# Moving one load and one store of a rotary kernel from SyncE's queue to GpSimd's

## The chip, the cores and the metric

One core of one Trainium2 chip. The metric is device time in microseconds (us) of one execution; executions of one kernel mostly agree within about 0.3%. "Faster" or "slower" means by more than 2%.

A word on names. Tile 0 to 3 are the four quarters of x, 8.39 MB each. "Load 1" brings tile 1 into on-chip memory, "store 1" takes it back. A "row" is what one partition contributes to one transfer: 64 KB for a whole tile, 32 KB for half a tile. Each of the 16 DMA engines carries 8 of the 128 rows of every transfer. A "hole" is time in which the DMA engines have nothing to move. A "packet record" is the trace's entry for one piece that a DMA engine moved: its queue, start, duration and size. "The software queue" is GpSimd's, "the hardware queue" is SyncE's.

## The reference

```python
def reference(x, cos, sin):          # x (16, 512, 16, 64), cos and sin (512, 32), float32
    x1, x2 = x[..., :32], x[..., 32:]
    cos = cos[None, :, None, :]; sin = sin[None, :, None, :]
    first  = x1[..., :16] * cos[..., :16] - x1[..., 16:] * sin[..., :16]
    second = x1[..., :16] * sin[..., :16] + x1[..., 16:] * cos[..., :16]
    return np.concatenate([first, second, x2], axis=-1)
```

x2, half of the data, only passes through: 33.55 MB in, 33.55 MB out, and little arithmetic.

## The kernel before

A ring of three slots of 64 KB per partition holds the tiles; tile 3 reuses the slot of tile 0, so load 3 must wait until store 0 has landed. VectorE rotates each tile in place, in two halves of K/2 = 8 positions. All x transfers are issued by SyncE, in one queue.

```python
    NS = 3; KC = K // 2; KL = 14
    ring = const_pool.tile([P, NS, K, H, D], fp32)

    def load(t, lo=0, hi=K):
        return nc.sync.dma_start(out=rows(t, lo, hi), in_=xf[t, :, lo * R : hi * R])
    def store(t, lo=0, hi=K):
        return nc.sync.dma_start(out=of[t, :, lo * R : hi * R], in_=rows(t, lo, hi))

    nc.gpsimd.dma_start(out=spread[:, 0, 0], in_=cosf)
    nc.gpsimd.dma_start(out=spread[:, 0, 1], in_=sinf)
    load(0)
    load(1)
    load(2, 0, KC)
    # ... VectorE spreads cos and sin over the partitions ...
    def rotate(t, lo, hi):
        # ... views x1, c, s, b_t ...
        nc.vector.tensor_mul(out=b_t, in0=x1, in1=s)
        nc.vector.tensor_mul(out=x1, in0=x1, in1=c)
        nc.vector.tensor_sub(...)
        nc.vector.tensor_add(...)
    def turn(t):
        rotate(t, 0, KC)
        rotate(t, KC, K)
        return store(t)

    turn(0)
    load(2, KC, K)
    near = load(3, 0, KL)
    load(3, KL, K)
    tc.add_manual_dep(turn(1).ins, near.ins.name, ...)   # store 1 waits for load 3
    turn(2)
    turn(3)
```

## Time and profile before

| | before |
|---|---|
| median of all its runs | 161.5 to 161.7 us |
| span in the trace | 160.33 us |
| DMA packets, share of 16 engines' span | 97.8% |
| VectorE busy | 70% |
| VectorE's last instruction ends | 130.58 us |
| last store lands | 159.29 us |

The prediction below shows the lines that carry this. Two more, from the waits and the DMA issues of the kernel before. In the first the columns are who waited, for whom, us in total, times, longest; in the second the transfer, the number of issues and the median us from issue to landing (KB each stands only where a transfer is not a whole tile):

```profile
DVE b_t L96 <- DMA ring<-in_x_dram: 1.9, 1, 1.9
```
```profile
out_dram<-ring SPq DMA_DIRECT2D x4, 25.6
```

VectorE waits for x once, for load 0, and never again: every later tile is there early. A store takes 25.6 us to land where its bytes alone need 19.5, since others stand before it in the queue.

### The profile page before, as it was taken

The page shows a single profiled execution, that of the slowest core. Times are in us where ns is not written, and L with a number is a line of the kernel's source. Part 1 is how long each engine was busy: PE and PEld are TensorE (multiplying, and loading weights), DVE is VectorE, ACT ScalarE, POOL GpSimd, SP SyncE. Part 2 cuts the span into 40 slices and gives each one's busy share as a digit, 9 for nine tenths or more (in the row PEclk, how much of TensorE's full clock was granted, in tenths as well). Part 3 has the DMA queues.
Part 4 walks back from the last instruction along what each step waited for, and adds up shares of the span by engine and source line. Part 5 has one row for each costly group of instructions (what it writes and reads, how often), then busy time and mean ns, then how long its engine had stood idle before and what let it go on. Part 6 is the DMA issues. An engine that isn't in the chain of part 4 may idle for free.

```text
span 160.3 us, 113 instructions
## 1 busy us (share of the span) xinstructions
DVE 112.4 (70%) x43; POOL 1.4 (1%) x6
## 2 busy tenths in 40 slices
DVE  1000959999999999999999999999999950000000
POOL 3000000000000000000000000000000000000000
DMA  7969969699699996999999995996996996996990
GB/s 262 540 262 540 491 294 523 278 507 491 294 392 441 474 523 262 523 392 392 499 482 458 458 444 253 546 523 262 523 523 262 523 507 278 523 507 278 523 507 16
DMA packets 1504, 67.24 MB, mean 419 GB/s; under 512 B 192, under 2 KB 192, under 8 KB 224
## 3 DMA queue, kind: packets, MB, share of 16 engines
q1 hardware_dynamic: 1440, 67.11, 97.6%
q0 software_dynamic: 64, 0.13, 0.2%
HBM read 33.69 MB, written 33.55 MB: 419 GB/s over the span
## 4 chain that ended last, share of the span: by engine, by line
DVE 59%; DMA 14%; issue 7%; DVEq 1%
DVE b_t L96 22%; DVE ring L97 22%; DMA ring<-in_x_dram 14%; DVE ring L101 10%; DVE ring L98 4%; DVEq L148 1%; DVEq L96 0%
## 5 line engine op out<-in xcount | busy, mean ns | idle before, releaser
L96 DVE TENSOR_TENSOR b_t<-ring,table 128x4096 f32<-128x4096 f32 x8 | 35.5, 4432 | 2.1 <-DMA ring<-in_x_dram 1.9
L97 DVE TENSOR_TENSOR ring<-ring,table 128x4096 f32<-128x4096 f32 x8 | 35.4, 4424 | 0.3
L98 DVE TENSOR_TENSOR ring<-ring,b_t 128x2048 f32<-128x2048 f32 x8 | 18.3, 2287 | 0.3
L101 DVE TENSOR_TENSOR ring<-ring,b_t 128x2048 f32<-128x2048 f32 x8 | 18.2, 2280 | 0.0
L73 DVE LOAD_MASK_SELECT spun<-stage x1 | 0.0, 14 | 14.4 <-DMA stage<-in_sin_dram 14.4
L83 DVE COPY table<-packed 32x1024 f32<-32x1024 f32 x4 | 2.7, 684 | 0.1
L80 DVE COPY packed<-spun 32x512 f32<-32x512 f32 (+3 forms) x4 | 1.7, 416 | 0.1
L61 DVE MEMSET stage<- 128x512 f32 x1 | 0.5, 485 | 0.9 <-PEq L137 0.9
L73 DVE STREAM_SHUFFLE spun<-stage 128x512 f32<-128x512 f32 x1 | 0.7, 723 | 0.0
L63 POOL DMA_DIRECT2D stage<-in_cos_dram x1 | 0.6, 649 | 1.3 <-DVE stage L61 1.3
L64 POOL DMA_DIRECT2D stage<-in_sin_dram x1 | 0.5, 532 | 0.0
L137 POOL MEMSET const-float32-0.0<- 128x1 f32 x1 | 0.1, 93 | 0.2 <-issue 0.2
L137 POOL MEMSET const-bfloat16-1.0<- 128x1 bf16 x1 | 0.1, 95 | 0.0
L137 POOL MEMSET const-uint8-127<- 128x1 uint8 x1 | 0.1, 93 | 0.0
L137 POOL MEMSET const-float32-1.0<- 128x1 f32 x1 | 0.1, 92 | 0.0
## 6 DMA issues: line engine op xcount, KB each, us to landing
ring<-in_x_dram SPq DMA_DIRECT2D x2, 4096.0 KB, 41.4
ring<-in_x_dram SPq DMA_DIRECT2D x1, 7168.0 KB, 26.4
ring<-in_x_dram SPq DMA_DIRECT2D x1, 1024.0 KB, 28.5
stage<-in_cos_dram POOLq DMA_DIRECT2D x1, 64.0 KB, 9.0
stage<-in_sin_dram POOLq DMA_DIRECT2D x1, 64.0 KB, 13.4
out_dram<-ring SPq DMA_DIRECT2D x4, 25.6
ring<-in_x_dram SPq DMA_DIRECT2D x2, 32.0
```

Of the source, the lines that this page charges most:

```text
L61: nc.vector.memset(stage[:, :, :, 0:Q], 0.0)
L63: nc.gpsimd.dma_start(out=spread[:, 0, 0], in_=cosf)
L64: nc.gpsimd.dma_start(out=spread[:, 0, 1], in_=sinf)
L73: nc.vector.stream_shuffle(out=spun[:], in_=stage.rearrange("p t k j -> p (t k) j")[:, :, 0:Q], mask=[j % PQ * REP for j in range(PB)],)
L80: nc.vector.tensor_copy(out=packed[0:n], in_=spun[q * PB : q * PB + n])
L83: nc.vector.tensor_copy(out=table[r * PB : (r + 1) * PB].rearrange("p t k c j -> p (t k) c j"), in_=packed.unsqueeze(2).to_broadcast((PB, ...
L96: nc.vector.tensor_mul(out=b_t, in0=x1, in1=s)
L97: nc.vector.tensor_mul(out=x1, in0=x1, in1=c)
L98: nc.vector.tensor_sub(out=x1[:, :, :, 0:Q], in0=x1[:, :, :, 0:Q], in1=b_t[:, :, :, Q:HF])
L101: nc.vector.tensor_add(out=x1[:, :, :, Q:HF], in0=x1[:, :, :, Q:HF], in1=b_t[:, :, :, 0:Q])
L137: nc = _bacc.Bacc("TRN2", target_bir_lowering=False, num_devices=1)
L148: with _tile.TileContext(nc) as tc:
```

## The change

The intent, as the text of the change says it: load 1 and store 2 go to GpSimd's queue, which leaves eight transfers on the hardware queue; load 1 starts when load 0 has landed, so that tile 2's first half runs ahead of it; tile 2's second half is kept behind store 0.

```diff
-    def load(t, lo=0, hi=K):
-        return nc.sync.dma_start(out=rows(t, lo, hi), in_=xf[t, :, lo * R : hi * R])
+    def load(t, lo=0, hi=K, queue=nc.sync):
+        return queue.dma_start(out=rows(t, lo, hi), in_=xf[t, :, lo * R : hi * R])
 # ... store() likewise ...
-    load(0)
-    load(1)
+
+    def behind(transfer, point, kind=mybir.DependencyClass.Sync):
+        tc.add_manual_dep(transfer.ins, point.ins.name,
+            mybir.DependencyInfo(kind, mybir.DependencyReason.DATA), reason="...")
+
+    first = load(0)
     load(2, 0, KC)
+    behind(load(1, queue=nc.gpsimd), first)
 # ...
-    def turn(t):
+    def turn(t, queue=nc.sync):
         rotate(t, 0, KC)
         rotate(t, KC, K)
-        return store(t)
+        return store(t, queue=queue)
 
-    turn(0)
-    load(2, KC, K)
+    head = turn(0)
+    behind(load(2, KC, K), head, mybir.DependencyClass.NoSync)
     near = load(3, 0, KL)
     load(3, KL, K)
 
-    tc.add_manual_dep(turn(1).ins, near.ins.name, ...)
-    turn(2)
+    behind(turn(1), near)
+    turn(2, nc.gpsimd)
     turn(3)
```

A `NoSync` dependence only fixes the order of issue; it waits for nothing.

More of the change, by code (lines that the diff above doesn't have):

```diff
@@ L52, in rows, with store @@
         return ring[:, t % NS, lo:hi].rearrange("p k h d -> p (k h d)")
-    def load(t, lo=0, hi=K):
-        return nc.sync.dma_start(out=rows(t, lo, hi), in_=xf[t, :, lo * R : hi * R])
-    def store(t, lo=0, hi=K):
-        return nc.sync.dma_start(out=of[t, :, lo * R : hi * R], in_=rows(t, lo, hi))
+    def load(t, lo=0, hi=K, queue=nc.sync):
+        return queue.dma_start(out=rows(t, lo, hi), in_=xf[t, :, lo * R : hi * R])
+    def store(t, lo=0, hi=K, queue=nc.sync):
+        return queue.dma_start(out=of[t, :, lo * R : hi * R], in_=rows(t, lo, hi))
     nc.vector.memset(stage[:, :, :, 0:Q], 0.0)
@@ L64 @@
     nc.gpsimd.dma_start(out=spread[:, 0, 1], in_=sinf)
-    load(0)
-    load(1)
+    def behind(transfer, point, kind=mybir.DependencyClass.Sync):
+        tc.add_manual_dep(
+            transfer.ins,
+            point.ins.name,
+            mybir.DependencyInfo(kind, mybir.DependencyReason.DATA),
+            reason="the transfer follows another at the DMA engines",
+        )
+    first = load(0)
     load(2, 0, KC)
+    behind(load(1, queue=nc.gpsimd), first)
     PQ = PB // REP
@@ L103, in rotate @@
         )
-    def turn(t):
+    def turn(t, queue=nc.sync):
         rotate(t, 0, KC)
         rotate(t, KC, K)
-        return store(t)
-    turn(0)
-    load(2, KC, K)
+        return store(t, queue=queue)
+    head = turn(0)
+    behind(load(2, KC, K), head, mybir.DependencyClass.NoSync)
     near = load(3, 0, KL)
     load(3, KL, K)
-    tc.add_manual_dep(
-        turn(1).ins,
-        near.ins.name,
-        mybir.DependencyInfo(mybir.DependencyClass.Sync, mybir.DependencyReason.DATA),
-        reason="the store follows the loads at the DMA engines",
-    )
-    turn(2)
+    behind(turn(1), near)
+    turn(2, nc.gpsimd)
     turn(3)
```

## The prediction

> **What bounds the kernel now.** The chain of waits is the usual first view, but here I read it second, because a kernel that only moves 67 MB has to be held against its transfer rate first. From the page, busy shares, transfer rows and queues:
>
> ```profile
> span 160.3 us, 113 instructions
> DVE 112.4 (70%) x43; POOL 1.4 (1%) x6
> DMA packets 1504, 67.24 MB, mean 419 GB/s; under 512 B 192, under 2 KB 192, under 8 KB 224
> q1 hardware_dynamic: 1440, 67.11, 97.6%
> q0 software_dynamic: 64, 0.13, 0.2%
> ```
>
> The reader is to see that VectorE works 112.4 of 160.3 us, while the packets of the two queues fill 97.6% + 0.2% = 97.8% of the sixteen DMA engines' span: 0.978 x 160.3 = 156.8 us. Only 3.5 us per engine are empty. Where? The same trace by stretches (columns: stretch, its length, VectorE's and GpSimd's busy time, clock, DMA share, rate; a packet counts wholly where it starts, so single shares can exceed 1):
>
> ```profile
> 0.00:2.00 2.00, 0.48 (x1) 0.49 (x5) 1.00 1.18 393
> 2.00:22.00 20.00, 5.14 (x10) 0.88 (x2) 1.00 0.90 387
> 22.00:50.00 28.00, 26.74 (x9) 0.00 (x0) 1.00 1.02 429
> 50.00:72.00 22.00, 21.86 (x6) 0.00 (x0) 1.00 0.99 430
> 120.00:140.00 20.00, 10.51 (x4) 0.00 (x0) 1.00 1.00 433
> 158.80:160.30 1.50, 0.00 (x0) 0.00 (x0) 1.00 0.00 0
> ```
>
> From 22 us on the rate is 429 to 433 GB/s with a share of about 1.0; the last 1.5 us move nothing, and by the packet records the first packet starts at 1.74 us (mean over the engines 2.0). 2.0 + 1.5 = 3.5: the empty time is all at the two ends. Then the chain and SyncE's waits, to see what VectorE has to do with it:
>
> ```profile
> 0.74 22.22 DMA ring<-in_x_dram
> 49.94 4.44 DVE b_t L96
> 128.38 2.20 DVEq L148
> ```
> ```profile
> SPq L58 <- DMA ring<-in_x_dram: 46.5, 2, 25.6
> SPq L148 <- DMA out_dram<-ring: 28.3, 1, 28.3
> SPq L55 <- DMA out_dram<-ring: 21.7, 1, 21.7
> ```
>
> The chain ends with VectorE at 130.58 us and hides the rest: after its last instruction SyncE still waits 28.3 us for a store. One 8.39 MB store at 430 GB/s is 19.5 us, so some 9 us of other transfers stood in front of it. VectorE has that slack before its end can move the end. From issue plus time to landing in the transfer view, and the semaphores: load 0 lands at 22.96, load 1 at 42.99, tile 2's first half at 52.76, store 0 at 72.45, tile 2's second half at 81.94, load 3's 7168 KB at 98.89 and its rest at 101.36, stores 1, 2, 3 at 120.72, 140.01, 159.29. Each follows the one before by its bytes over 430 GB/s: one unbroken queue.
>
> **What the Trainium skill says.** First, "DMA: Bandwidth & Descriptors", section "Where 436 GB/s comes from": 16 ports at 27.2 GB/s make 435.2 GB/s. The trace agrees: a packet of 65,536 B has a median of 2,418 ns, 27.1 GB/s per engine, 433.6 for sixteen. Second, same page, "Queues, rings and completion order": each DMA engine alternates between the queues that have work, a whole packet from each. The trace agrees: on the engine whose packets they are, the packet of the cosines starts at 17.76 - 10.46 = 7.3 us (taking off the trace's zero), then a 64 KB packet, then its 4 B semaphore packet at 9.87, then a 64 KB packet, then the sines. Third, same page, "SWDGE vs HWDGE vs iDMA": GpSimd's descriptors are written by software into rings, packets are preferably up to 4096 B and at most 64 descriptors. The trace shows GpSimd packets of 4,096 B for two 2 KB rows; it shows none with 64 KB rows, so how such a row is cut is the open point. Fourth, "SBUF - State Buffer", section "SBUF: two separate sides": VectorE in a two-port mode can keep GpSimd from writing descriptors. No run shows it yet; here VectorE was idle when GpSimd issued (14.4 us waiting for the sines).
>
> **The change part by part.** No byte and no arithmetic goes away. VectorE's 41 rows stand in the same order; GpSimd gains two transfers, SyncE falls from ten to eight.
>
> Floor first: 8 tiles x 8 rows of 64 KB per engine = 64 rows x 2.418 = 154.75 us. Add 2.0 at the start, 1.5 at the end, 0.3 for cosines and sines (2 x 0.168), some 0.7 for the first rows (about 3.1 instead of 2.4 us) and 0.7 for slow rows of load 1 between 24 and 48 us: 159.95, against 160.33 measured. So the order of transfers can gain only slow rows, under 1 us (0.6%), as long as the engines stay fed; it can lose whatever it leaves empty.
>
> (a) Load 1 moves behind load 0's landing, onto GpSimd's queue; tile 2's first half (eight rows of 32 KB per engine, 1.213 us each, 9.7 us) fills the engines from about 22.4 to 32. GpSimd needs the semaphore, its issue (0.65 us for the cosines) and about 1 us to the first packet (SyncE: 0.74 to 1.74), so load 1's rows start at about 25, when two of the eight rows are gone. If a 64 KB row is one packet, the six others alternate with six of load 1: 6 x (1.21 + 2.42) = 21.8 us, to 46.8; two more rows of load 1 take 4.8, to 51.6, landing about 52.5. The check by bytes: the same 20.97 MB must pass, and before the last of them landed at 52.76. VectorE wants load 1 at 49.94, so it now waits about 2.6 us, up to 5 if rows of store 0, issued at 49.94, cut in before the last row and its semaphore packet.
>
> (b) Store 0 and then tile 2's second half stay in SyncE's queue in that order: store 0 lands at 72.4, the second half at 82, load 3 at 98.9 and 101.4, all set by bytes sent. Were the half ahead of the store, store 0 and load 3's issue would each come 9.7 us later; the ordering dependence avoids that and so keeps the status quo.
>
> (c) Store 1 is released by load 3 at 98.9 as before. Store 2 is released by VectorE at 104.1 + 2.6 = 106.7 and alternates with store 1 instead of standing behind it: store 1 lands about 133 instead of 120.7, store 2 about 145 instead of 140. No one waits for either but the end.
>
> (d) VectorE ends at 130.6 + 2.6 = 133.2 (at worst 135.6). Store 3 needs about 1 us to its first packet, and the engines have work until 140: 5.8 us (3.4 at worst) remain of the slack. Nothing runs empty; store 3's last byte passes at 158.9 and lands at 159.3.
>
> (e) The eight hardware transfers save two SyncE issues of 0.33 to 0.43 us, all under running transfers: 0.
>
> Sum: span 160.3 + 0 from order, -0.7 to +0.5 for slow rows and the software path. With the 1.36 us between 160.33 and the median 161.69: **161.7 us**.
>
> **The rivals.** Small packets: were a 64 KB row cut into 4,096 B packets (159 ns each), load 1 would get one such packet per 32 KB row, then run alone from about 32 us; 128 packets x 0.159 = 20.4 us leave some six to eight when store 0's rows arrive, each then waiting 2.42 us: landing about 66, VectorE 15 us late, its end at 146, store 3's 19.4 us after that: span near 168, 169 us measured. For it: the one packet size seen on this queue. Against it: those two rows were 2 KB, so this may just be their sum. I give it 7%.
>
> Whole transfers as packets: were eight rows one packet, load 1 would pass in one go and land at 45 to 48, VectorE would not wait, and the end would still be the queue's: 161.7.
>
> Descriptors late: VectorE starts its first tile at 23.05, just when GpSimd writes load 1's descriptors. One blocked instruction of 4.43 us gives 27.5, still before the half tile runs out at 32. Only a block beyond 32 leaves engines empty, us for us; over 2% needs until 35. The multiplies take 4.43 us for 4096 elements, about one element a cycle, no sign of a faster two-port mode. 3%.
>
> Two queues help: if rows from two queues hid what slows rows now, there is at most 0.7 us in load 1's rows, plus part of the 0.3 us skew at the end: 160.7. Nothing approaches 2%.
>
> **Range and chances.** Faster by 2% would need 158.5 measured, a span of 157.1, which is 2.8 us below the 159.95 summed above: 2%. Slower by 2% needs 164.9: the small packets, late descriptors, or a slower software path (2% on a quarter of the bytes is only 0.8 us): 10%. The rest, 88%, is the same. Range 160.9 to 163.0, wider upward because empty engines are the only sizeable effect.
>
> **What would show it.** Right: software packets of 65,536 B at about 2.42 us; a share of about a quarter of the bytes (16.9 of 67.2 MB) on the software queue; load 1 landing at 52 to 55; VectorE idle 2 to 5 us before tile 1, ending at 133 to 136; a rate of 429 to 433 GB/s from 22 us to 158. Wrong: software packets of 4 KB, VectorE waiting over 9 us, or a stretch with a DMA share well under 1 between 25 and 158 us. If engine shares stay at 1 but packets grow longer, the software path itself costs; if the end comes earlier than 159, rows have become shorter, which I hold unlikely.

## The result and the profile after

| | before | after |
|---|---|---|
| median, same rounds (6 runs each) | 161.70 us | 162.09 us |
| ratio | | 1.0024, 95% interval 1.0011 to 1.0037 |
| span in the trace | 160.33 us | 160.30 us |
| load 1 lands | 42.99 us | 52.05 us |
| VectorE's end | 130.58 us | 132.79 us |
| stores 1, 2, 3 land | 120.72, 140.01, 159.29 | 130.46, 144.95, 159.41 |

A ratio is the mean time of one kernel's fast runs over that of the other's of the same rounds, so it is not quite the ratio of the medians. 0.24% slower is clear of the noise, and the trace's spans do not show it. The experiments look for it.

The page of the changed kernel:

```profile
DVE 112.4 (70%) x43; POOL 2.5 (2%) x8
...
DMA packets 1504, 67.24 MB, mean 419 GB/s; under 512 B 192, under 2 KB 192, under 8 KB 224
...
q1 hardware_dynamic: 1152, 50.33, 73.6%
q0 software_dynamic: 352, 16.91, 24.4%
```

A quarter of the bytes has moved to the software queue, in as many packets as before: its 256 packets of 65,536 B have a median of 2,418 ns in the packet records, exactly what they took on the hardware queue. The queues together fill 98.0% where they filled 97.8%. The stretches, as before:

```profile
22.00:50.00 28.00, 26.69 (x8) 0.55 (x1) 1.00 1.04 449
50.00:72.00 22.00, 19.72 (x6) 0.00 (x0) 1.00 0.98 405
120.00:140.00 20.00, 12.71 (x4) 0.00 (x0) 1.00 1.04 452
158.80:160.30 1.50, 0.00 (x0) 0.00 (x0) 1.00 0.00 0
```

No share is well under 1 before the last stretch. (A packet counts wholly where it starts, so 449 and 405 GB/s are edge effects of the cut at 50 us; together they make 430.) VectorE is busy 2.1 us less between 50 and 72 us and 2.2 us more between 120 and 140: it starts tile 1 later and has the room. The chain of waits and the waits of VectorE and SyncE:

```profile
23.28 28.77 DMA ring<-in_x_dram
...
52.14 4.45 DVE b_t L106
...
130.59 2.20 DVEq L153
```
```profile
DVE b_t L106 <- DMA ring<-in_x_dram: 4.0, 2, 2.2
```
```profile
SPq L153 <- DMA out_dram<-ring: 26.0, 2, 14.3
SPq L55 <- DMA out_dram<-ring: 20.1, 1, 20.1
```

The chain looks very different from before: it gives 32% to loads of x, where before it gave 14%. The time has hardly moved. That is the warning in this profile: the chain is followed back from the last instruction, which is VectorE's at 132.79, while the last store lands at 159.41. It explains when VectorE ends, and VectorE's end does not set the time.

The DMA issues of GpSimd show the two moved transfers:

```profile
ring<-in_x_dram POOLq DMA_DIRECT2D x1, 28.8
out_dram<-ring POOLq DMA_DIRECT2D x1, 38.8
```

38.8 us for a store whose bytes need 19.5: it shares the engines with store 1 and then with store 3, and only the end of the program waits for it.

### The profile page after: what moved, and what is told of

Read it like the earlier page. It is cut to its first block, busy times and chain, and to the rows that moved or that the text cites. A ratio compares the mean times of both kernels' runs of the same rounds, so it can differ in the third digit from the quotient of the medians.

```text
span 160.3 us, 114 instructions
## 1 busy us (share of the span) xinstructions
DVE 112.4 (70%) x43; POOL 2.5 (2%) x8
## 4 chain that ended last, share of the span: by engine, by line
DVE 43%; DMA 32%; issue 6%; DVEq 1%
DMA ring<-in_x_dram 32%; DVE b_t L106 17%; DVE ring L107 17%; DVE ring L111 7%; DVE ring L108 3%; DVEq L153 1%; DVEq L106 0%
## 5 line engine op out<-in xcount | busy, mean ns | idle before, releaser
L58 POOL DMA_DIRECT2D out_dram<-ring x1 | 0.5, 542 | 82.4 <-DVE ring L111 82.4
L55 POOL DMA_DIRECT2D ring<-in_x_dram x1 | 0.6, 551 | 20.4 <-DMA ring<-in_x_dram 20.4
```

What stands on the lines that cost most here:

```text
L55: return queue.dma_start(out=rows(t, lo, hi), in_=xf[t, :, lo * R : hi * R])
L58: return queue.dma_start(out=of[t, :, lo * R : hi * R], in_=rows(t, lo, hi))
```

## The experiments

Three questions were open. Which part of the change costs the 0.24%? How near is VectorE's lateness to the end? What are the two ordering dependences worth? The theory at the outset was the prediction's: the engines are the bound, order is neutral while they stay fed. In the packet records of the changed kernel one thing stood out: store 0's first rows, one on each engine, start at 51.04 to 51.64 us and take 3.1 to 3.5 us, where nearly all others take 2.42. Summed as (duration minus 2.418) over 16 engines this "excess" is 0.88 us. At that moment load 1 had just run out on GpSimd's queue, and SyncE's queue had been empty since tile 2's first half landed at 44.80. I called this the cold-queue theory. Rivals: VectorE's late start costs, or the software store near the end does.

A third, that the two queues taking turns slow each other's rows, the trace settles: the rows that start from 26 to 48.5 us, load 1's and, until 44.80, tile 2's beside them, have an excess of 0.00 us.

The twelve runs were made in three groups of four, in the order below, each group on a chip of its own; each group shares the runs of the kernel before, whose medians were 161.61, 161.57 and 161.51 us. So where a run of the second or third group is set against the change's 162.12 us of the first, the difference between the chips is about 0.1 us at most.

**The change again, unaltered.**

> The changed kernel unaltered, on the chip of the next three. All theories: 161.9 to 162.3 us, ratio 1.001 to 1.004, because the 0.4 us was clear of noise before. If the ratio falls within 0.001 of 1, the difference was the chip's and not the change's. Cold-queue theory: the first rows of store 0 again take about 3.3 us where all other rows take 2.42.

Measured: 162.12 us against 161.61, ratio 1.0031 (1.0018 to 1.0043). The loss is real, and the excess at 51 us is there again, 0.87 us.

**Load 1 alone on GpSimd's queue.**

```diff
-    turn(2, nc.gpsimd)
+    turn(2)
```

> Only load 1 on GpSimd's queue behind load 0; tile 2's store back on SyncE. Cold-queue theory (store 0 finds SyncE's queue empty, its first rows take 0.9 us longer): all of the loss is here, 161.9 to 162.3 us, first rows of store 0 about 3.3 us. Software-end theory (the extra time comes with a software store near the end): equal to before, 161.6 to 161.8 us. VectorE waits 2 to 2.5 us for load 1 in both.

Measured: 162.18 us, ratio 1.0033 (1.0020 to 1.0045); excess at 51 us 0.86 us. All of the loss is in load 1's move.

**The new order, all on SyncE's queue.**

```diff
-    behind(load(1, queue=nc.gpsimd), first)
+    behind(load(1), first, mybir.DependencyClass.NoSync)
 # ...
-    turn(2, nc.gpsimd)
+    turn(2)
```

> The changed order (load 0, half of tile 2, load 1) but all x transfers on SyncE's queue. Load 1 lands at about 52.5 and VectorE waits about 2.5 us, as in the change. Cold-queue theory: store 0 stands behind load 1 in the same queue, its first rows take 2.42 us, and the time is that of before, 161.5 to 161.8 us. Rival: the loss comes from VectorE's late start or from store 0 coming only about 1 us before the loads run out, whichever queue holds them: 161.9 to 162.3 us and slow first rows here too.

Measured: 161.59 us, ratio 1.0001 (0.9985 to 1.0016). Load 1 lands at 52.16. The stretch from 50.90 to 51.90 us, first of the changed kernel, then of this one, holds the start of store 0's first row on each of the 16 engines; with a stretch of 1 us, the DMA share is the mean duration of those rows in us:

```profile
50.90:51.90 1.00, 0.00 (x0) 0.00 (x0) 1.00 3.30 1049
```
```profile
50.90:51.90 1.00, 0.00 (x0) 0.00 (x0) 1.00 2.43 1049
```

The same 16 rows of the same store start at the same time (1049 GB/s is 16 x 64 KB in 1 us), and take 3.30 us there and 2.43 here. Store 0 was issued at 49.97 there and at 50.07 here, so it was not later there. And VectorE's wait is the same as in the changed kernel:

```profile
DVE b_t L106 <- DMA ring<-in_x_dram: 4.1, 2, 2.2
```

So VectorE's lateness and the new order cost nothing; that load 1 runs out on another queue than the one store 0 comes on does.

SyncE shows something at this handover too. Of the changed kernel, and below it the same instruction's durations (minimum, median, maximum in ns) with all on SyncE:

```profile
50.37 2.21 SPq L55 DMA_DIRECT2D ring<-in_x_dram  x1
```
```profile
L55 SPq DMA_DIRECT2D ring<-in_x_dram x6: 328/425/443, 0.7 to 72.2; - x6
```

The issue right behind store 0's, of tile 2's second half, took 2.21 us in the changed kernel, and began before the slow rows did. It took 2.2 to 2.4 us in its second trace and with load 1 alone on GpSimd. But it took 2.71 us in the next run but one, which has no slow rows at 51 us, so it is a companion of the handover and no explanation of the slow rows.

**Store 2 alone on GpSimd's queue.**

```diff
-    load(2, 0, KC)
-    behind(load(1, queue=nc.gpsimd), first)
+    load(1)
+    load(2, 0, KC)
```

> Loads as before, all on SyncE; only tile 2's store on GpSimd's queue. Cold-queue theory: equal to before, 161.5 to 161.8 us; load 1 lands at 43, VectorE never waits for it; store 1 lands at about 130 and store 2 at about 143 instead of 121 and 140, without effect on the end. Software-end theory: 161.9 to 162.3 us.

Measured: 161.51 us, ratio 0.9992 (0.9980 to 1.0005). Store 1 lands at 132.13, store 2 at 144.21. No effect, as expected; the software-end rival falls.

**Store 0 cut in two, to keep SyncE's queue filled.**

```diff
-    def turn(t, queue=nc.sync):
+    def turn(t, queue=nc.sync, split=False):
         rotate(t, 0, KC)
+        if split:
+            store(t, 0, KC)
         rotate(t, KC, K)
-        return store(t, queue=queue)
+        return store(t, KC if split else 0, K, queue=queue)
 # ...
-    head = turn(0)
+    head = turn(0, split=True)
```

> The changed kernel with store 0 cut in two: its first eight rows of 16 leave as soon as they are rotated, at about 36.6 us, so SyncE's queue still has work when load 1 runs out on GpSimd's. Cold-queue theory: the slow rows at 51 us (0.87 us) are gone and the time falls to 161.1 to 161.6 us, although load 1 lands later (53 to 56) and VectorE waits 3 to 6 us for it. Rival (late VectorE is what costs): it gets slower, 162.5 us or more.

Measured: 163.56 us, ratio 1.0130 (1.0109 to 1.0150): 1.3% longer, a clear miss. The time lies where the rival put it (162.5 us or more), but not because any lateness costs: the run with all on SyncE showed that 2.2 us of it is free. The excess at 51 us is gone, but load 1 lands only at 58.31, and from tile 0's end at 50.01 VectorE waits 8.4 us for it:

```profile
DVE b_t L106 <- DMA ring<-in_x_dram: 10.2, 2, 8.4
```

So VectorE ends at 139.04, store 3 finds nearly dry engines (excess 0.38 us at 140 us, and some 0.4 us more skew between the engines at the end than in the changed kernel). Besides, 32 of load 1's rows, started between 41 and 47 us, took 3.1 to 3.4 us, 1.71 us of excess in all, around the time at which SyncE's queue passes from load rows to store rows. I have no theory of these that the runs test.

**Load 1 without its wait for load 0.**

```diff
-    nc.gpsimd.dma_start(out=spread[:, 0, 1], in_=sinf)
+    sines = nc.gpsimd.dma_start(out=spread[:, 0, 1], in_=sinf)
 # ...
-    behind(load(1, queue=nc.gpsimd), first)
+    behind(load(1, queue=nc.gpsimd), sines, mybir.DependencyClass.NoSync)
```

> The changed kernel with load 1 issued right behind the sines instead of behind load 0's landing. Both queues' 64 KB rows alternate from about 17 us, so load 0 lands near 27.8 instead of 23; VectorE ends tile 0 near 54.8; the loads still run out at about 51.6, so the engines stand empty for 4 to 5 us before store 0: 165.5 to 167.5 us. If the order of arrival did not matter to the end (slack theory without the hole): 162.

Measured: 168.66 us, ratio 1.0436 (1.0420 to 1.0452), 1.2 us above the expected range. Load 0 lands at 30.31 (expected 27.8), tile 0 is rotated at 57.3. Stretches of this kernel:

```profile
22.00:50.90 28.90, 20.36 (x6) 0.00 (x0) 1.00 1.00 433
...
51.60:58.00 6.40, 6.33 (x4) 0.00 (x0) 1.00 0.00 0
58.00:75.00 17.00, 16.90 (x5) 0.00 (x0) 1.00 1.00 432
```

A hole of 6.4 us and more, with full rate on both sides; the packet records give 6.8 us per engine. It is larger than the 4 to 5 expected by as much as load 0 came later, and it passes into the time: 168.66 - 162.12 = 6.5. The first rows of store 0 after this hole:

```profile
57.90:58.90 1.00, 1.00 (x1) 0.00 (x0) 1.00 2.48 1049
```

They come 0.85 us after the issue at 57.28 and take 2.48 us, though SyncE's queue had been empty for over 6 us. So an empty queue alone does not make its first rows slow. This is what a violation of the prediction's condition "as long as the engines stay fed" looks like, and what the wait for load 0 buys.

**Tile 2's second half without its place behind store 0.**

```diff
-    behind(load(2, KC, K), head, mybir.DependencyClass.NoSync)
+    load(2, KC, K)
```

> The changed kernel without the ordering that keeps tile 2's second half behind store 0; the scheduler then places it at the start. Store 0 lands at about 82 instead of 72.7, and load 3 waits for it with nothing else queued: a hole of about 0.5 (landing) + 1.0 (issue to first packet) + 0.9 (cold first row) = 2.4 us near 82, less the cold rows at 51 that it removes: 163 to 164.5 us. If only bytes count: 161.6 to 162.1.

Measured: 164.63 us, ratio 1.0186 (1.0173 to 1.0200), 0.13 us above the expected range; between "same" and "slower", the verdict is "unclear". Tile 2's second half was issued at 1.64 us, so load 1 shares the engines with both halves and lands at 56.30, too. Store 0 lands at 82.12, load 3 is issued at 82.14. The packet records show 1.9 us of empty engines there, and the first rows of load 3 carry 0.72 us of excess; together 2.6 us, against 2.5 us more than the changed kernel (164.63 - 162.12). The excess at 51 us is gone, as expected, but 1.0 us of slow rows stands at 58 to 60 us instead.

**A small transfer behind load 1.**

```diff
-    behind(load(1, queue=nc.gpsimd), first)
+    second = load(1, queue=nc.gpsimd)
+    behind(second, first)
 # ... after the tables are built:
+    pad = nc.gpsimd.dma_start(out=stage.rearrange("p t k j -> p (t k j)"), in_=xf[0, :, 0:R])
+    behind(pad, second, mybir.DependencyClass.NoSync)
```

> The changed kernel with a transfer of 0.52 MB (reloaded x into the spent staging buffer; results unchanged) behind load 1 on GpSimd's queue: 8 packets of 4 KB, 1.27 us more per engine. Lateness theory (the small packets fill the time in which store 0's first row is not ready): cold excess falls from 0.87 us by half or more, total 162.4 to 162.8 us. Emptiness theory (the first row on an empty hardware queue is slow whatever else runs): excess stays near 0.87 us, total 163.2 to 163.6 us.

Measured: 162.81 us, ratio 1.0084 (1.0069 to 1.0099): 0.7 us over the change, not 1.27, and 0.01 above the range of the lateness theory; two of the five runs (163.18 and 163.31) came near or into the range of the other theory. Store 0's first rows are no longer slow; the small packets run first and carry an excess of 0.44 us themselves. About half of the loss is filled with other work, as the lateness theory says; the median and the vanished slow row speak against emptiness alone (163.2 to 163.6). That store 0's first row was "not yet ready" in that time is a reading of this, not shown: after an empty stretch the first row comes 0.85 us after its issue (load 1 without its wait), and here, as in the changed kernel, store 0 had been issued for longer than that when load 1 ran out.

**VectorE 4.43 us longer.**

```diff
-        nc.vector.tensor_mul(out=b_t, in0=x1, in1=s)
+        for _ in range(2 if (t, lo) == (1, 0) else 1):
+            nc.vector.tensor_mul(out=b_t, in0=x1, in1=s)
```

> The changed kernel with tile 1's first multiply done twice: VectorE 4.43 us longer, its end near 137.2 instead of 132.8. Slack theory: the other transfers keep the engines busy until about 139.7, so nothing moves: 162.0 to 162.7 us. If VectorE is on the path that sets the end: 166.5 us.

Measured: 163.22 us, ratio 1.0102 (1.0087 to 1.0118): 1.1 us over the change, 0.5 us above what I allowed. VectorE lets store 3 go at 137.34, 1.7 us before GpSimd's store runs out at 139.0, and yet:

```profile
138.90:139.90 1.00, 0.00 (x0) 0.00 (x0) 1.00 3.32 1049
```

That is the same handover a second time: an empty SyncE queue, a software transfer that has just run out, and store 3's first rows at 3.32 us. Here it is store to store, so a change of direction is not needed for it; and store 3 had been issued 1.7 us before, so a late issue is not needed either.

**VectorE 8.86 us longer** (the same edit, with 3 in place of 2).

> The same multiply done three times: VectorE 8.86 us longer, its end near 141.7. Slack theory: the engines run empty at about 139.7 and store 3's first packet comes 1.0 us after its issue, at 142.7: 2.5 to 3.5 us of empty engines, 165.0 to 166.0 us. If VectorE were on the path: 171. If there were slack left: 162.

Measured: 165.30 us, ratio 1.0229 (1.0212 to 1.0246), within the expected range. The stretch in which the engines wait for VectorE:

```profile
139.80:142.00 2.20, 1.81 (x1) 0.00 (x0) 1.00 0.00 0
```

The packet records give 3.2 us of hole; 165.30 - 162.12 = 3.2. Store 3's first rows after it are not slow, 2.46 us (issued at 141.63, started at 142.47). Of 8.86 us on VectorE 5.7 are hidden.

**Tile 2's second half ahead of store 0, at tile 0's end.**

```diff
-    head = turn(0)
-    behind(load(2, KC, K), head, mybir.DependencyClass.NoSync)
+    rotate(0, 0, KC)
+    done = rotate(0, KC, K)          # rotate() returns its last instruction
+    half = load(2, KC, K)
+    behind(half, done)
+    behind(store(0), half, mybir.DependencyClass.NoSync)
```

> The changed kernel with tile 2's second half issued at tile 0's end but ahead of store 0, so that at 51 us SyncE's empty queue starts with load rows (32 KB, 1.21 us otherwise) and not with store rows. Empty-queue theory: these first rows carry the excess of about 0.9 us as store 0's did. Turn-of-direction theory (loads to stores costs it): no excess at 51, some 0.4 to 0.9 us at 61 when store 0 follows. In both store 0 lands at about 82, a hole of 2 to 2.5 us follows there as in the run without the ordering, and the total is 163.5 to 165 us.

Measured: 165.45 us, ratio 1.0244 (1.0229 to 1.0259), 0.45 above the range. Load rows at the handover are slow at 51 us too (0.41 us of excess, 34% of a 32 KB row; store 0's had 36% of a 64 KB row), which the turn-of-direction theory denied; the other theory had expected some 0.9. An excess that is half as large for half the bytes does not look like a fixed time of not being ready. But slow rows of 1.3 us in all stand at 58 to 61 us as well, before store 0, more than either theory said. The hole at 82 us is 2.0 us. So neither theory accounts for all slow rows.

**The kernel before, for a second trace.**

> The kernel before, unaltered, for a second trace and as a control of the method: ratio 0.998 to 1.002. If the slow rows of load 1 between 24 and 48 us (0.87 us per engine in the first trace) belong to the kernel they stand there again; if they are an event of that one execution, they are elsewhere or gone, and then the change did not gain by removing them.

Measured: 161.54 us against 161.51, ratio 1.0002 (0.9987 to 1.0017). The slow rows of load 1 between 24 and 48 us are gone; 0.39 us of excess stands at 67 to 73 us instead, and the last store lands at 158.65, not 159.29. The first trace of the kernel before was of a somewhat long execution (162.1 us; the runs of its comparison took 161.58 to 161.88, and this one 161.47). That is why the two first traces seemed to have equal spans.

With it the 0.24% closes fairly well. Excess of all x rows that start after 5 us, in us per engine by the packet records, one trace each:

| kernel | excess | of it at 51 us | median us |
|---|---|---|---|
| before, first trace (execution of 162.1) | 0.91 | 0.00 | 161.70 |
| before, second trace | 0.42 | 0.00 | 161.54 |
| new order, all on SyncE | 0.72 | 0.01 | 161.59 |
| store 2 alone on GpSimd | 0.44 | 0.01 | 161.51 |
| load 1 alone on GpSimd | 1.06 | 0.86 | 162.18 |
| the change | 1.03 | 0.88 | 162.09 |
| the change again | 1.04 | 0.87 | 162.12 |

Without the first row (a long execution) the three kernels with load 1 on SyncE average 0.53 us and 161.55 us, the others 1.04 us and 162.13 us: 0.5 us of excess for 0.6 us of time. The change swaps 0.4 to 0.7 us of slow rows elsewhere for 0.87 us at the handover. This closing rests on one or two traces per kernel.

No version beat both kernels by more than noise; store 2 alone on GpSimd's queue (0.9992, interval up to 1.0005) is not distinguishable from before.

## Why the prediction was right

- **The bound.** Right: span set by bytes at 27.1 GB/s per engine. Holes pass into the time nearly one for one (6.8 us of hole for 6.5 us of time; 3.2 for 3.2).
- **(a) Load 1.** Right but for small sizes: packets of 65,536 B at 2,418 ns; tile 2's first half at 44.80 (predicted 46.8) because the first software row started at 27.0, not 25, 3.7 us after its issue. The prediction had taken SyncE's 1 us for it, while its own trace showed 5.6 us for the cosines (issued at 1.70, first packet at 7.30); load 1 at 52.05 (52.5); VectorE's new wait 2.2 us (2.6). Store 0's rows did not cut in.
- **(b) Store 0 and the half tile.** Right: store 0 landed at 72.70. Without the ordering it landed at 82.12, 9.4 us later (9.7 worked out). What that would cost was not said: 2.5 us.
- **(c) and (d).** Right: store 1 at 130.46 (133), store 2 at 144.95 (145), VectorE's end at 132.79 (133.2). The term that was too generous is the rest of the slack, 5.8 us: it counted only with a hole. At 4.43 us there was none, and the handover's slow rows made it cost 1.1 us; at 8.86 us 5.7 were hidden.
- **(e) Eight transfers.** The change itself saved nothing by having fewer; this was not isolated further.
- **The sum.** "-0.7 to +0.5 for slow rows and the software path" held the true +0.4 to +0.5 by luck, since the named sources were wrong: the software path's rows cost nothing, and the 0.7 us in load 1's rows belonged to one execution. In their place stands the handover at 51 us, which the prediction did not foresee. It asked whether the engines run empty, and not whether the next queue's first row comes at full speed when the other one runs out. The step to the clock was wrong as well: 1.36 us sets the span of one long execution (162.10 us) against the median of others. Within one execution of the kernels in the table, time minus span is 1.77 to 1.80 us (162.10 - 160.33, 162.07 - 160.30). And the trace counts 43 VectorE instructions, not 41; nothing rests on that.
- **The rivals.** Small packets did not occur, nor whole transfers as packets. Load 1's first row came about 2 us later than worked out, with no hole; whether its descriptors were late, and why, no run isolates. VectorE did not hold up the issue itself: load 1 was issued at 23.28 us, beside the multiply of 23.09, in 0.55 us, like the sines with VectorE idle (0.54).

**Left open.** That the loss goes with load 1's queue and stands in the rows at the handover is shown; its mechanism is not. Why are first rows slow right behind the other queue's last row, even 1.7 us after their issue (VectorE 4.43 us longer), while they are not in the same queue after 0.9 us (new order, all on SyncE), nor after a hole of 3.2 or 6.8 us? After the holes of 1.9 and 2.0 us at 82 us they are slow again (0.72 us in the run without tile 2's place). And what are the slow rows that appear once or more in most traces (0.4 us at 67 to 73, 1.0 at 58 to 60, 1.7 at 41 to 47), often near a turn between loads and stores?

## What to carry to other kernels

When the DMA engines are full from start to end, as here, expect from splitting transfers over queues a change in who lands when, and little in the time; first add up rows times their measured duration, and see how little is left to win. What order can do is lose: look for every moment at which only one more transfer stands between the engines and a hole, and have the next one queued before that; in the same queue it cost nothing here. Check what the remedy delays, though: filling that moment with half of store 0 removed the slow rows and made the whole 0.9% longer than the change. And where the chain of waits ends well before the last landing, read it as a statement about that engine and not about the time.

## What the Trainium skill lacked or had wrong

- "DMA: Bandwidth & Descriptors", section "SWDGE vs HWDGE vs iDMA": packets of at most 4096 B are called preferred, and the passage does not say what becomes of longer rows. Here a 64 KB row on GpSimd's queue was one packet of 65,536 B, 2,418 ns, like on SyncE's queue, and so it takes turns with the hardware queue's rows one for one.
- Same page, "Queues, rings and completion order": it says how an engine alternates while both queues have work, not what a handover costs. Here the first row on the hardware queue, just as the software queue runs out, took 3.30 us for 2.42 (0.87 us per engine), and 2.43 in the same queue. After holes of 6.8 and 3.2 us, on an empty queue, it took 2.48 and 2.46. So a second queue, which brought nothing (ratio 0.9992 for store 2), can lose a little (1.0033 for load 1).
